# Channel mixer as seven block products instead of eight, with activations through DRAM

## The chip, the cores and the metric

The kernel runs on one core of a Trainium2 chip. The metric is the device time of one execution in microseconds. TensorE (PE) multiplies, VectorE (DVE), ScalarE (ACT) and GpSimd (POOL) work on elements, SyncE (SP) issues nearly all DMAs. Each engine takes its instructions in the order of its own queue.

## What is computed

One encoder layer and a final norm are applied to two sequences with the same weights, one of 512 tokens (short) and one of 1024 (long). Everything is float32.

```python
u = rms_norm(x, norm1_g)
proj = u @ w_in
...                                        # Fourier mixing and retention branches, gated and merged
x = x + merged @ w_out
u2 = rms_norm(x, norm2_g)
h_gate, h_val = jnp.split(u2 @ w_up, 2, axis=-1)          # 1024 -> 2 x 2816
h_conv = hp[:, :-2] * conv_w[0] + hp[:, 1:-1] * conv_w[1] + hp[:, 2:] * conv_w[2] + conv_b
x = x + (jax.nn.gelu(h_conv, approximate=False) * h_val) @ w_down   # 2816 -> 1024
y = rms_norm(x, final_norm_g)
```

`hp` is `h_gate` padded by one token at both ends. The change concerns the part from `u2` on, the channel mixer.

## The kernel before

Activations lie with the features on partitions and 512 tokens on the free axis. There are three such token tiles t: 0 is the short sequence, 1 and 2 are the long one. Each feature block k has 128 features, so D_MODEL is KD = 8 blocks and D_FF is FF = 22.

Each float32 operand is split into two parts of a shorter format, h (a ScalarE cast) and l (VectorE's subtraction `x - h`), by `split`, L71 and L72. `mm3` (L105 to L107) makes one product of 128 x 128 weights with 512 columns from three matmuls, hh, lh and hl. Weights come as slabs of 128 x 1024 (`wslab`): one DMA into `wr` and one split.

The merge runs over token tiles in the order 1, 2, 0: eight projections with w_ret_proj (RP), then eight with w_out (WO), each of 24 matmuls. `norm2` then makes the 16 split operands u2 of a token tile; it runs between the next tile's projections (`pend`).

The mixer runs over two groups, tiles (1, 2) and then tile 0. `up` makes one of the 22 feature blocks: the gate slab, the convolution (L786, L793, L796), the Gelu, the value slab, the product (L804) and its split. `down` takes two such blocks at a time, multiplies them by all eight output blocks and adds the result to y (L851); in the group's last call it also makes the squares for the final norm. `final` (L823) scales y and stores it. A down call stands in the code between the two up calls of the next pair, so that TensorE has other products while an activation is made. A scheduler orders the instructions of all engines by priority and by its own estimate of when each can run; the order is fixed when the program is built. Pools have a number of buffers; a tile waits for the buffer's earlier user.

Of the kernel before, what the change touches and what calls it, by code (L numbers as in the profile page):

```python
# [14 lines left out]
P = 128  # L15
# [10 lines left out]
SL_RP, SL_WO, SL_UP, SL_DN = 44, 52, 60, 104  # L26
N_SLABS = 126
# [6 lines left out]
def emit(ctx, tc, x, wsl, wfour, tab, cst, rcst, vec, out):  # L34
# [4 lines left out]
    upool = ctx.enter_context(tc.tile_pool(name="u", bufs=24))  # L39
# [34 lines left out]
    state = {}  # L74
# [29 lines left out]
    def mm3(o, lh, ll, rh, rl, first, last):  # L104
        nc.tensor.matmul(o, lh, rh, start=first, stop=False)  # L105
        nc.tensor.matmul(o, ll, rh, start=False, stop=False)  # L106
        nc.tensor.matmul(o, lh, rl, start=False, stop=last)  # L107
# [46 lines left out]
    # ------------------------------------------------------------- norm 1 and the mixers  # L154
    wpool = ctx.enter_context(tc.tile_pool(name="w", bufs=4, reuse_waits="tile"))
# [71 lines left out]
    # Fourier: channel DFT token-major, then the sequence DFT of the lower half of the frequencies  # L227
# [123 lines left out]
    # decays: per-head tables from the logits  # L351
# [139 lines left out]
    # retention, two heads at a time; the small steps run between thirds of the projections  # L491
# [225 lines left out]
    ntp = ctx.enter_context(tc.tile_pool(name="nt", bufs=4, reuse_waits="tile"))  # L717
    state["tmp"] = ntp, "nt", 4
    mp = cctx.enter_context(tc.tile_pool(name="mh", bufs=KD, side="right", reuse_waits="tile"))
    u2 = [None] * 3  # L720

    def norm2(t, xs, ss):
        r = rstd_cols(ss.acc)
        yield
        ps = rstd_rows(r)
        u2[t] = ([], [])
        for k in range(KD):
            s = tmp("xn")
            nc.vector.scalar_tensor_tensor(s, xs[k], vc[:, V_G2 + k:V_G2 + k + 1], ps, op0=ALU.mult, op1=ALU.mult)  # L729
            xs[k] = None  # L730
            h, l = utile("uh"), utile("ul")
            u2[t][0].append(h)
            u2[t][1].append(l)
            split(h, l, s)

    pend = None
    for it, t in enumerate(order):
        mh, ml = [], []
        for n in range(KD):
# [34 lines left out]
    pool = {}

    def up(gi, j):
        dp = pool["d"]
        ts = groups[gi]
        n = len(ts) * TC
        w = wslab(SL_UP + 2 * j)  # L780
        hc = dp.tile([P, 2 * TC], F32, name="hc", tag="hc", bufs=2)
        cw = [vc[:, V_CW + 3 * j + i:V_CW + 3 * j + i + 1] for i in range(3)]
        hps = []
        for i, t in enumerate(ts):
            ps = proj(w, u2[t])
            nc.scalar.activation(hc[:, i * TC:(i + 1) * TC], ps, AF.Identity,  # L786
                                 bias=vc[:, V_CB + j:V_CB + j + 1], scale=cw[1])
            hps.append(ps)
        for i, ps in enumerate(hps):
            o = i * TC  # L790
            e = min(o + TC + 1, n)
            s = hc[:, o + 1:e]
            nc.vector.scalar_tensor_tensor(s, ps[:, :e - o - 1], cw[0], s, op0=ALU.mult, op1=ALU.add)  # L793
            b = max(o - 1, 0)
            s = hc[:, b:o + TC - 1]
            nc.vector.scalar_tensor_tensor(s, ps[:, b + 1 - o:TC], cw[2], s, op0=ALU.mult, op1=ALU.add)  # L796
        nc.scalar.activation(hc[:, :n], hc[:, :n], AF.Gelu)
        w = wslab(SL_UP + 2 * j + 1)
        al = dp.tile([P, 2 * TC], F32R, name="al", tag="al", bufs=3)
        ah = dp.tile([P, 2 * TC], F32R, name="ah", tag="ah", bufs=3)  # L800
        for i, t in enumerate(ts):
            ps = proj(w, u2[t])
            m = slice(i * TC, (i + 1) * TC)
            nc.vector.tensor_tensor(hc[:, m], ps, hc[:, m], op=ALU.mult)  # L804
        split(ah[:, :n], al[:, :n], hc[:, :n])
        return ah, al

    def final(t, m, ss, fast):
# [7 lines left out]
        rr = pool["d"].tile([P, 2 * TC], F32, name="hc", tag="hc", bufs=2)[:, :cols]  # L816
        nc.scalar.copy(rr, ps[:, :cols])
        for n in range(KD):
# [3 lines left out]
            else:  # L822
                nc.gpsimd.tensor_tensor(y, y, rr, op=ALU.mult)  # L823
            nc.sync.dma_start(out[t, n, :, m], y)

    late = []

    def tick():
        for it in list(late):
            if next(it, late) is late:  # L830
                late.remove(it)

    def down(gi, b, acts):
        dp = pool["d"]
        ts = groups[gi]
        ws = [wslab(SL_DN + 2 * b + i) for i in range(2)]
        last = b == FF // 2 - 1
        units = [(i * TC, t, slice(0, TC)) for i, t in enumerate(ts)]
        if last and gi:
            units = [(0, 0, slice(0, TC // 2)), (TC // 2, 0, slice(TC // 2, TC))]  # L840
        for o, t, tm in units:
            cols = tm.stop - tm.start
            m = slice(o, o + cols)
            ss = SumSq()
            for n in range(KD):
                c = slice(n * P, (n + 1) * P)
                ps = bank(cols)
                for q in range(2):
                    mm3(ps, ws[q][0][:, c], ws[q][1][:, c], acts[q][0][:, m], acts[q][1][:, m], q == 0, q == 1)
                y = ys[t, n][:, tm]  # L850
                nc.vector.tensor_tensor(y, ps, y, op=ALU.add)  # L851
                if last:
                    ss.add(y)
                    nc.scalar.activation(y, y, AF.Identity, scale=vc[:, V_GF + n:V_GF + n + 1])
                if n % 2 or last:
                    tick()
# [4 lines left out]
    for gi in range(2):  # L861
        for b in range(FF // 2):
# [11 lines left out]
            if todo:  # L874
                down(*todo)
# [114 lines left out]
```

## Time and profile before

| what | us |
|---|---|
| median of 3 runs (lowest, highest) | 2377.97 (2377.53, 2379.83) |
| span of the profiled execution | 2379.3 |
| its time beside the span | no separate time is listed; the span lies inside the range of the runs |
| TensorE busy | 2340.7 |
| VectorE busy | 1192.4 |
| ScalarE busy | 651.3 |
| GpSimd busy | 368.4 |

The page gives the busy time of each engine, its share of the span and the number of instructions. Below it and in the groups, a row has the line in the kernel, the engine, the operation, out<-in by the program's names with shapes, the count, the busy time and the mean duration in ns, and the idle time ahead with what ended it. In a row by stretches, the columns are the length, then the busy time and the count of each engine, then TensorE's granted clock, the share of the DMA engines and GB/s. Rows in order of time have the start, the duration, the engine and the instruction.

### The profile page before, as it was taken

What the parts mean: (1) busy time and instruction counts of PE and PEld (TensorE: products, weight loads), DVE (VectorE), ACT (ScalarE), POOL (GpSimd) and SP (SyncE); (2) the same over time, 40 slices, a digit from 0 to 9 for tenths busy, and PEclk for the clock granted to TensorE, in tenths of its full rate; (3) what the DMA queues carried; (4) which work ended last, traced back from release to release, by engine and by line L of the source; (5) the groups of instructions that cost most, each with busy time, mean ns of one, the idle gap of its engine ahead of it and who ended that gap; (6) DMA issues with size and microseconds to landing.
All of it is one profiled execution on the core that took longest, in us unless ns stands there. A gap on an engine that the chain in (4) does not pass through costs nothing.

```text
span 2379.3 us, 27499 instructions
## 1 busy us (share of the span) xinstructions
PE 2340.7 (98%) x10898; PEld 1918.6 (81%) x10898; DVE 1192.4 (50%) x2144; ACT 651.3 (27%) x1007; POOL 368.4 (15%) x200
## 2 busy tenths in 40 slices
PE   8899999999999999999999999999999999999997
PEld 6788888888888888877878788888888888788886
DVE  7454435656555642456543643444443446555555
ACT  6242222222222212234332211112211215322323
POOL 3799401212111110101100000000000002200000
PEclk9999999999999999999999999999999999999999
DMA  5252220201011123557453111111111113423231
GB/s 182 72 165 89 81 70 1 80 1 54 27 45 36 40 81 115 186 183 236 144 185 119 48 50 45 42 48 53 48 50 45 47 51 114 143 89 106 89 98 62
DMA packets 76593, 203.46 MB, mean 86 GB/s; under 512 B 8496, under 2 KB 11824, under 8 KB 76464
## 3 DMA queue, kind: packets, MB, share of 16 engines
q1 hardware_dynamic: 73008, 195.41, 26.0%
q10 hardware_dynamic: 3456, 6.29, 0.7%
q8 instruction: 86, 1.41, 0.2%
q14 instruction: 43, 0.35, 0.0%
HBM read 170.21 MB, written 31.46 MB: 85 GB/s over the span
## 4 chain that ended last, share of the span: by engine, by line
PE 87%; DVE 3%; DMA 2%; ACT 2%; POOL 1%; issue 1%; SPq 0%; POOLq 0%; ACTq 0%; DVEq 0%
PE bank L105 27%; PE bank L106 27%; PE bank L107 27%; DMA wr<-wsl 2%; PE bank L616 1%; DVE wl L72 1%; PE bank L562 1%; PE bank L573 1%; PE bank L569 1%; ACT wh L71 1%; POOL y L823 1%; DMA og<-og 1%; PE bank L551 1%; PE bank L638 0%; DVE xn L729 0%
## 5 line engine op out<-in xcount | busy, mean ns | idle before, releaser
L105 PE MATMUL bank<-uh,wh 128*128 128x512 f32 x1728 | 688.3, 398 | 5.0 <-ACT wh L71 5.0
L107 PE MATMUL bank<-ul,wh 128*128 128x512 f32 x1728 | 683.9, 396 | 0.0
L106 PE MATMUL bank<-uh,wl 128*128 128x512 f32 x1728 | 683.2, 395 | 0.2 <-DVE wl L72 0.2
L71 ACT CAST wh<-wr 128x1024 fp32r<-128x1024 f32 (+3 forms) x256 | 258.1, 1017 | 743.9 <-PE bank L107 626.5
L105 PEld LDWEIGHTS bank<-uh,wh 128*128 128x128 f32 x1728 | 325.4, 188 | 79.1 <-ACT wh L71 5.0
L106 PEld LDWEIGHTS bank<-uh,wl 128*128 128x128 f32 x1728 | 325.4, 188 | 75.8 <-DVE wl L72 1.2
L107 PEld LDWEIGHTS bank<-ul,wh 128*128 128x128 f32 x1728 | 325.2, 188 | 75.6
L72 DVE TENSOR_TENSOR wl<-wr,wh 128x1024 fp32r<-128x1024 f32 (+3 forms) x256 | 313.2, 1231 | 95.1 <-ACT wh L71 93.4
L851 DVE TENSOR_TENSOR y<-bank,y 128x512 f32<-128x512 f32 (+1 forms) x272 | 178.8, 674 | 115.3 <-PE bank L107 114.3
L105 PE MATMUL bank<-ah,wh 128*128 128x512 f32 (+1 forms) x544 | 211.9, 390 | 1.0 <-DVE y L851 0.7
L106 PE MATMUL bank<-ah,wl 128*128 128x512 f32 (+1 forms) x544 | 211.0, 388 | 1.1 <-DVE wl L72 1.1
L107 PE MATMUL bank<-al,wh 128*128 128x512 f32 (+1 forms) x544 | 210.2, 387 | 0.0
L129 POOL TENSOR_TENSOR nr<-nv,mhalf 128x4 f32<-128x4 f32 (+1 forms) x10 | 11.9, 1194 | 1180.1 <-DVE nv L128 1149.8
L793 DVE SCALAR_TENSOR_TENSOR hc<-bank,vc,hc 128x512 f32<-128x512 f32 (+1 forms) x66 | 47.5, 748 | 260.3 <-ACT hc L786 260.3
L420 POOL TENSOR_TENSOR D<-two,D 128x64 f32<-128x64 f32 x16 | 170.3, 10675 | 0.0
L105 PE MATMUL bank<-wh,uh 128*128 128x512 f32 x384 | 166.8, 434 | 0.0
L106 PE MATMUL bank<-wh,ul 128*128 128x512 f32 x384 | 151.6, 395 | 0.0
L107 PE MATMUL bank<-wl,uh 128*128 128x512 f32 x384 | 151.2, 394 | 0.0
L804 DVE TENSOR_TENSOR hc<-bank,hc 128x512 f32<-128x512 f32 x66 | 45.6, 692 | 171.4 <-PE bank L107 170.1
L786 ACT ACTIVATE hc<-bank,vc 128x512 f32<-128x512 f32 x66 | 51.4, 779 | 273.5 <-PE bank L107 273.5
L105 PEld LDWEIGHTS bank<-ah,wh 128*128 128x128 f32 x544 | 102.3, 188 | 24.5 <-DVE y L851 1.1
L106 PEld LDWEIGHTS bank<-ah,wl 128*128 128x128 f32 x544 | 102.3, 188 | 23.9 <-DVE wl L72 1.8
(172 smaller groups left out, 2861.4 us busy)
## 6 DMA issues: line engine op xcount, KB each, us to landing
wr<-wsl SPq DMA_DIRECT2D x222, 512.0 KB, 3.7
wr<-tab SPq DMA_DIRECT2D x18, 516.0 KB, 3.7
xs<-x SPq DMA_DIRECT2D x24, 256.0 KB, 4.7
sb<-sg ACTq DMA_DIRECT2D x24, 256.0 KB, 2.0
ma<-sg SPq DMA_DIRECT2D x24, 256.0 KB, 2.0
og<-sg SPq DMA_DIRECT2D x24, 256.0 KB, 2.4
og<-og SPq DMA_DIRECT2D x24, 256.0 KB, 3.9
uh<-x SPq DMA_DIRECT2D x24, 256.0 KB, 4.0
```

What stands on the lines that cost most here:

```text
L71: nc.scalar.copy(h, src)
L72: nc.vector.tensor_tensor(l, src, h.bitcast(F32), op=ALU.subtract)
L105: nc.tensor.matmul(o, lh, rh, start=first, stop=False)
L106: nc.tensor.matmul(o, ll, rh, start=False, stop=False)
L107: nc.tensor.matmul(o, lh, rl, start=False, stop=last)
L420: nc.gpsimd.tensor_tensor(D[:, m], two.broadcast_to([P, 64]), D[:, m], op=ALU.pow)
L551: nc.tensor.transpose(tp[:, i * P:(i + 1) * P], r[:, i * P:(i + 1) * P], ident)
L562: nc.tensor.matmul(sp, kT, qbd.rearrange("p h n -> p (h n)"), start=True, stop=True)
L786: nc.scalar.activation(hc[:, i * TC:(i + 1) * TC], ps, AF.Identity, bias=vc[:, V_CB + j:V_CB + j + 1], scale=cw[1])
L793: nc.vector.scalar_tensor_tensor(s, ps[:, :e - o - 1], cw[0], s, op0=ALU.mult, op1=ALU.add)
L804: nc.vector.tensor_tensor(hc[:, m], ps, hc[:, m], op=ALU.mult)
L851: nc.vector.tensor_tensor(y, ps, y, op=ALU.add)
```

## The change

A product of two matrices cut into 2 x 2 blocks is made from seven block products and 15 block sums instead of eight products (Winograd's form). The blocks of the weights are halves of the contraction and halves of the outputs. The blocks of the activations are halves of the contraction and halves of the tokens: for the long sequence, tiles 1 and 2; for the short one, columns 0 to 255 and 256 to 511.

- `u_ops(k)` loads x2 of the long sequence again, scales it, and makes seven split operands for block pair k and k+4 (A11, A12, A22, S1 to S4). Blocks 0 and 1 run in the third merge's RP part, 2 in its WO part, 3 behind it. `u_ops0(k)` does that for the short sequence.
- `w_ops` loads one 128 x 2048 slab (w_up's gate and value blocks for one j, both contraction halves) and makes three sums and the splits, so that seven weight operands are there. They are made anew for each sequence.
- `quad` runs the seven products into three banks and hands the results to a `sink` as they come. `quads` chains jobs: the first product of a job stands ahead of the last two of the job before.
- The long sequence runs its 22 up jobs first. `spill_pair` stores two activations and their four sums in DRAM (`da` to `dd`). Then the down projection runs in four groups of 2, 3, 3 and 3 pairs, four jobs each; `act_ops` loads and splits seven operands for each pair, and the sinks add to y.
- The short sequence then runs 22 up jobs with 256 columns, keeps all activations, and its down projection runs by output block over 20 activations, then the last two by half tiles as before.
- The finals of the long sequence run between the short one's up jobs, one scaling per step.

```diff
+OPS = ("A11", "S1", "S2", "A12", "S3", "S4", "A22")
+DN_GROUPS = ((0, 2), (2, 5), (5, 8), (8, 11))
...
+    def w_ops(src, w):
+        raw = wp.tile([P, 2048], F32, name="wr", tag="wr", bufs=2)[:, :4 * w]
+        nc.sync.dma_start(raw, src)
...
+        b11, b21 = hl(raw[:, :2 * w], 2)
+        ta = wp.tile([P, 1024], F32, name="wt", tag="wt", bufs=2)[:, :2 * w]
+        nc.vector.tensor_tensor(ta.rearrange("p (b c) -> p b c", b=2), b[:, 2:4], b[:, 0:3:2], op=ALU.subtract)
+        t1, t3 = hl(ta, 2)
+        tb = wp.tile([P, 1024], F32, name="wt", tag="wt", bufs=2)[:, :2 * w]
+        nc.vector.tensor_tensor(tb[:, :w], b[:, 3], ta[:, :w], op=ALU.subtract)
+        nc.vector.tensor_tensor(tb[:, w:], b[:, 1], tb[:, :w], op=ALU.subtract)
+        t2, t4 = hl(tb, 2)
+        b22, = hl(b[:, 3], 1)
...
+    def quad(w, act, cols, sink):
+        a = bank(cols)
+        product(a, w, act, "A11", start=True)
+        sink("P1", a)
+        yield
+        c = bank(cols)
+        product(c, w, act, "S1", start=True)
+        product(a, w, act, "S2")
+        sink("P1+P6", a)
+        b = bank(cols)
+        product(b, w, act, "A12", start=True)
+        sink("P2", b)
+        product(a, w, act, "S3")
+        sink("P1+P6+P7,P5", (a, c))
+        yield
+        product(c, w, act, "S4")
+        sink("P5+P3", c)
+        product(a, w, act, "A22")
+        sink("P1+P6+P7+P4", a)
+        yield
...
+    def spill_pair(j, a):
...
+        nc.sync.dma_start(d[0], a0[:, lo])
+        nc.sync.dma_start(d[1], a1)
+        s12 = tp.tile([P, 2 * TC], F32, name="v", tag="v")
+        nc.vector.tensor_tensor(s12[:, lo], a0[:, hi], a1[:, hi], op=ALU.add)
+        nc.vector.tensor_tensor(s12[:, hi], s12[:, lo], a0[:, lo], op=ALU.subtract)
+        nc.sync.dma_start(d[2], s12)
+        s34 = tp.tile([P, 2 * TC], F32, name="v", tag="v")
+        nc.vector.tensor_tensor(s34[:, lo], a0[:, lo], a0[:, hi], op=ALU.subtract)
+        nc.vector.tensor_tensor(s34[:, hi], a1[:, lo], s12[:, hi], op=ALU.subtract)
+        nc.sync.dma_start(d[3], s34)
...
+    for _ in quads([up_job(tp, j, uop, TC, spill_pair) for j in range(FF)]):
+        pass
...
+    def act_ops(p):
+        ops = {}
+        for name in OPS:
+            l, h = optile(p % 4), optile(p % 4)
+            nc.sync.dma_start(l.bitcast(F32), opd[p][name])
+            nc.scalar.copy(h, l.bitcast(F32))
+            nc.vector.tensor_tensor(l, l.bitcast(F32), h.bitcast(F32), op=ALU.subtract)
...
+    state["tmp"] = yp, "nt", 4
...
+    def u_ops0(k):
...
+        for kk in (k, k + 4):
+            v = tmp("x0")
+            nc.sync.dma_start(v, x2_d[kk][0])
+            nc.vector.scalar_tensor_tensor(v, v, vc[:, V_G2 + kk:V_G2 + kk + 1], rr[0], op0=ALU.mult, op1=ALU.mult)
...
+        s12, s34 = tmp("s12"), tmp("s34")
...
+    for _ in quads(down_jobs()):
+        pass
+    for k in range(4):
+        u_ops0(k)
+    for t in (1, 2):
+        late.append(final((yp, "fr", 1), t, slice(0, TC), state["sums"][t], ()))
...
+    for j, _ in enumerate(quads([up_job(t0p, j, uop0, H, keep) for j in range(FF)])):
...
```

The order of the instructions changes nearly everywhere in the mixer. Three places matter here.

VectorE in the short sequence's up projection. Before, two feature blocks and the down call of the pair before them take eight y sums, four more slabs and two chains of convolution, product (L804) and split (`al`):

```order
L851 TENSOR_TENSOR y<-bank,y 128x512 x8
L72 TENSOR_TENSOR wl<-wr,wh 128x1024 x2
L793 SCALAR_TENSOR_TENSOR hc<-bank,vc,hc 128x511
L796 SCALAR_TENSOR_TENSOR hc<-bank,vc,hc 128x511
L72 TENSOR_TENSOR wl<-wr,wh 128x1024
L804 TENSOR_TENSOR hc<-bank,hc 128x512
L72 TENSOR_TENSOR wl<-wr,wh 128x1024
L72 TENSOR_TENSOR al<-hc,ah 128x512
```

After, one job, thus one feature block, has these and two more (a 256-wide sink L953 and the split `w4l`); L804, L807 and L808 are the sums of weight blocks, L948 and L951 sinks, L959 the product:

```order
L804 TENSOR_TENSOR wt<-wr 128x1024
L75 TENSOR_TENSOR wl<-wr,wh 128x1024
L932 SCALAR_TENSOR_TENSOR hc<-g,vc,hc 128x511
L807 TENSOR_TENSOR wt<-wr,wt 128x512
L933 SCALAR_TENSOR_TENSOR hc<-g,vc,hc 128x511
L948 TENSOR_TENSOR g<-bank,g 128x256
L808 TENSOR_TENSOR wt<-wr,wt 128x512
L75 TENSOR_TENSOR wl<-wt,wh 128x1024
L959 TENSOR_TENSOR hc<-v,hc 128x512
L951 TENSOR_TENSOR v<-bank,v 128x256
L75 TENSOR_TENSOR wl<-wt,wh 128x1024
L75 TENSOR_TENSOR al<-hc,ah 128x512
```

The y sums are gone from this stretch, and weight splits and sums of weight blocks stand in their place.

VectorE between the long and the short sequence. Before, the last y sums and squares of the long one mix with the short one's first slabs and its first feature block:

```order
L851 TENSOR_TENSOR y<-bank,y 128x512
L72 TENSOR_TENSOR wl<-wr,wh 128x1024
L152 TENSOR_TENSOR sq<-sq 128x512 x2
L72 TENSOR_TENSOR wl<-wr,wh 128x1024
L793 SCALAR_TENSOR_TENSOR hc<-bank,vc,hc 128x511
L796 SCALAR_TENSOR_TENSOR hc<-bank,vc,hc 128x511
L804 TENSOR_TENSOR hc<-bank,hc 128x512
```

After, the first block of `u_ops0` (L1069 the scaling, L1076 to L1079 the sums, L75 the splits) follows on the last y sums (L1029) and some weight work, and three more such blocks follow on it:

```order
L808 TENSOR_TENSOR wt<-wr,wt 128x512
L1069 SCALAR_TENSOR_TENSOR x_15319<-x_15319,vc,rr_8230 128x512
L1069 SCALAR_TENSOR_TENSOR x_15322<-x_15322,vc,rr_8230 128x512
L75 TENSOR_TENSOR op<-x_15319,op 128x256
L1076 TENSOR_TENSOR s_15328<-x_15319,x_15322 128x256
L1078 TENSOR_TENSOR s_15329<-x_15319 128x256
L1077 TENSOR_TENSOR s_15328<-s_15328,x_15319 128x256
L1079 TENSOR_TENSOR s_15329<-x_15322,s_15328 128x256
L75 TENSOR_TENSOR op<-s_15328,op 128x512
L75 TENSOR_TENSOR op<-x_15322,op 128x512
L75 TENSOR_TENSOR op<-s_15329,op 128x512
L1069 SCALAR_TENSOR_TENSOR x_15346<-x_15346,vc,rr_8230 128x512
```

The four blocks stand behind the long sequence's last sum; no other work stands between them.

SyncE's queue between the long up and the long down projection. Before there is no such border; the loads of y stand between stores of x2 and slabs at the start of the mixer:

```order
L88 DMA wr<-wsl 128x1024
L766 DMA xx_0_167<-uh 128x512
L88 DMA wr<-wsl 128x1024
L873 DMA y<-xx_1_150 128x512
L766 DMA xx_0_170<-uh 128x512
L873 DMA y<-xx_1_153 128x512
```

After, loads of operands (`op`) stand among stores of the last pair and ahead of the 16 loads of y, of which the first three are shown:

```order
L1047 DMA op<-db_10469 128x512
L977 DMA db_10505<-hc 128x1024
L1047 DMA op<-dd_10471 128x512
L981 DMA dc_10506<-v 128x1024
L985 DMA dd_10507<-v 128x1024
L1047 DMA op<-dd_10471 128x512
L1057 DMA y<-xx_1_150 128x512
L1057 DMA y<-xx_1_162 128x512
L1057 DMA y<-xx_2_151 128x512
```

The operands of the first group now share the queue with stores that wait for VectorE and with the loads of y.

More of the change, by code (lines that the diff above doesn't have):

```diff
@@ new lines, in emit, with tick, quads @@
+    late = []
+    def tick():
+        for it in list(late):
+            if next(it, late) is late:
+                late.remove(it)
+    def quads(jobs):
+        prev = None
+        for prep, act, cols, sink, after in jobs:
+            w = prep()
+            g = quad(w, act, cols, sink)
+            next(g)
+            if prev:
+                next(prev[0])
+                prev[1]()
+                tick()
+            next(g)
+            tick()
+            prev = g, after
+            yield
+        next(prev[0])
+        prev[1]()
+        tick()
@@ L767, in emit @@
             ss.add(xr)
-            xs.append(xr)
-        pend = norm2(t, xs, ss)
-    groups = ((1, 2), (0,))
-    ys = {}
[L774 to L806, printed above, removed]
@@ L808, in final, with dspill @@
-    def final(t, m, ss, fast):
+            if pend and next(pend, 0) == 0:
+                pend = None
+        if it < 2:
+            pend = chain(norm2(t, ss), *((u_ops(0), u_ops(1)) if it else ()))
+    for _ in pend or ():
+        pass
+    mctx.close()
+    homes[3] = right("opc", 14, occtx)
+    for _ in u_ops(3):
+        pass
+    late.append(norm2(0, ss))
+    nctx.close()
+    def dspill(name, cols):
+        return dram.tile([P, cols], F32, name=name, tag=name)
+    opd = []
+    for p in range(FF // 2):
+        first, second, s12, s34 = dspill(f"da{p}", TC), *(dspill(f"d{x}{p}", 2 * TC) for x in "bcd")
+        opd.append({"A11": first, "A12": second[:, :TC], "A22": second[:, TC:], "S1": s12[:, :TC],
+                    "S2": s12[:, TC:], "S3": s34[:, :TC], "S4": s34[:, TC:], "tiles": (first, second, s12, s34)})
@@ L822, in final @@
             else:
-                nc.gpsimd.tensor_tensor(y, y, rr, op=ALU.mult)
+                nc.gpsimd.tensor_tensor(y, y, rw, op=ALU.mult)
             nc.sync.dma_start(out[t, n, :, m], y)
[L826 to L856, printed above, removed]
-            if last:
-                late.append(final(t, tm, ss, range(5) if gi else ()))
@@ new lines, in down_jobs @@
+    def down_jobs():
+        sums = None
+        for gi, (p0, p1) in enumerate(DN_GROUPS):
+            pairs = [act_ops(p) for p in range(p0, p1)]
+            act = {name: [o[name] for o in pairs] for name in OPS}
+            if gi == len(DN_GROUPS) - 1:
+                sums = {1: SumSq(rr[1]), 2: SumSq(rr[2])}
+            for q in range(4):
+                yield down_job(gi, q, act, sums)
+        state["sums"] = sums
+    for _ in quads(down_jobs()):
+        pass
+    for k in range(4):
+        u_ops0(k)
@@ new lines, in emit, with keep @@
+    for t in (1, 2):
+        late.append(final((yp, "fr", 1), t, slice(0, TC), state["sums"][t], ()))
+    occtx.close()
+    obctx.close()
+    actx = ExitStack()
+    t0p = right("t0", 2, actx)
+    ap = [(right("act", 22, actx), "act", 22), None, (opa, "op", 28)]
+    acts = [None] * FF
+    def keep(j, a):
+        pool, tag, bufs = ap[0 if j < 11 else 1 if j < 20 else 2]
+        l, h = (pool.tile([P, TC], F32R, name=x, tag=tag, bufs=bufs) for x in ("al", "ah"))
+        split(h, l, a)
+        acts[j] = h, l
@@ new lines, in emit @@
+    ws = [wslab(SL_DL + i) for i in range(2)]
+    for m in (slice(0, H), slice(H, TC)):
+        ss = SumSq()
+        for n in range(KD):
+            c = slice(n * P, (n + 1) * P)
+            ps = bank(H)
+            for q in range(2):
+                mm3(ps, ws[q][0][:, c], ws[q][1][:, c], acts[20 + q][0][:, m], acts[20 + q][1][:, m],
+                    q == 0, q == 1)
+            y = ys[0, n][:, m]
+            nc.vector.tensor_tensor(y, ps, y, op=ALU.add)
+            y_done(0, n, m, ss)
+            tick()
+        late.append(final((opa, "op", 28), 0, m, ss, range(5)))
```

271 lines of the change are left out of this document (215 added, 56 removed).

## Prediction

> **What bounds the kernel now.** I read the page first, then the busy time by stretches, then TensorE's own rows in the channel mixer.
>
> ```profile
> span 2379.3 us, 27499 instructions
> ...
> PE 2340.7 (98%) x10898; PEld 1918.6 (81%) x10898; DVE 1192.4 (50%) x2144; ACT 651.3 (27%) x1007; POOL 368.4 (15%) x200
> ```
> ```profile
> core 0: us, PE busy (x) PEld busy (x) DVE busy (x) ACT busy (x) POOL busy (x), PEclk, DMA share, GB/s
> 1249.26:2351.19 1101.93, 1099.81 (x4753) 889.08 (x4752) 520.53 (x660) 276.78 (x326) 28.47 (x19) 1.00 0.23 71
> 1160.00:1204.60 44.60, 44.60 (x201) 36.38 (x201) 28.51 (x37) 15.91 (x22) 12.31 (x8) 1.00 0.59 190
> 1204.60:1249.26 44.66, 43.72 (x188) 34.75 (x186) 20.84 (x25) 12.99 (x17) 0.00 (x0) 1.00 0.47 153
> 1400.00:1900.00 500.00, 500.00 (x2153) 404.32 (x2152) 210.17 (x268) 98.06 (x105) 0.00 (x0) 1.00 0.15 48
> ```
>
> From 1249.26 us, where the mixer's up projection starts, to 2351.19, where the last half-width unit starts, TensorE has 1099.81 of 1101.93 us and VectorE 520.53, under half. So this stage costs what its matmuls cost, and the price of one is the distance between two starts, not the mean duration, which overlaps its neighbour:
>
> ```profile
> 1249.26 0.39 PE L105 MATMUL bank<-uh,wh 128*128 128x512 f32 x1
> ...
> 1254.85 0.40 PE L105 MATMUL bank<-uh,wh 128*128 128x512 f32 x1
> ```
> ```profile
> 2351.19 0.28 PE L105 MATMUL bank<-ah,wh 128*128 128x256 f32 x1
> ...
> 2359.25 0.28 PE L107 MATMUL bank<-al,wh 128*128 128x256 f32 x1
> ```
>
> The first pair is 24 matmuls of 512 columns apart: 0.2329 us each; 2153 in 500 us give 0.2322. I use 0.2325. The second pair is 67 matmuls of 256 columns apart: 0.120 us each, though each loads its own weights.
>
> **The change, part by part.** VectorE's prices come from the mixer's groups:
>
> ```profile
> L851 DVE TENSOR_TENSOR y<-bank,y 128x512 f32<-128x512 f32 x256 | 172.5, 690 | 114.1 <-PE bank L107 113.1
> L72 DVE TENSOR_TENSOR wl<-wr,wh 128x1024 fp32r<-128x1024 f32 x123 | 150.2, 1234 | 31.4 <-ACT wh L71 31.4
> ...
> L796 DVE SCALAR_TENSOR_TENSOR hc<-bank,vc,hc 128x511 f32<-128x511 f32 x41 | 30.6, 746 | 0.8
> ...
> L72 DVE TENSOR_TENSOR al<-hc,ah 128x512 fp32r<-128x512 f32 x22 | 15.3, 694 | 2.1 <-ACT ah L71 2.1
> ...
> L851 DVE TENSOR_TENSOR y<-bank,y 128x256 f32<-128x256 f32 x16 | 6.3, 420 | 1.2 <-PE bank L107 1.2
> ...
> L72 DVE TENSOR_TENSOR ul<-xn,uh 128x512 fp32r<-128x512 f32 x8 | 5.1, 688 | 0.0
> L729 DVE SCALAR_TENSOR_TENSOR xn<-uh,vc,bank 128x512 f32<-128x512 f32 x6 | 4.1, 744 | 0.0
> ```
>
> Widths between these go by the 0.54 us that 512 more columns cost: 768 takes 0.96, 384 takes 0.55.
>
> *Matmuls, the gain.* Before, the mixer has 3 token tiles x (44 x 8 + 22 x 8) x 3 = 4752 matmuls of 512 (the last 96, of half width, counting as 48). The long sequence's up projection goes from 2112 to 22 x 84 = 1848: 264 x 0.2325 = 61.4 us less. Its down projection goes from 1056 to 924: 30.7 us less. The short sequence's up projection goes from 1056 of 512 columns (245.5 us) to 1848 of 256 (1848 x 0.120 = 221.8): 23.7 us less. Its down projection keeps its count. Together 115.8 us, all on TensorE, which sets the end. What follows takes part of it back.
>
> *The long up job.* One job is 84 x 0.2325 = 19.5 us of TensorE. VectorE has three 1024-wide splits and one difference of that width (4 x 1.23), a 512 split and two 512 differences (2.07), three sinks (2.07), two 1023-wide steps of the convolution (0.746 + 0.53 each by the slope from 512 to 1024, 2.6), a 1024 product (1.23), and half of four 512-wide sums for the stores (1.4): 14.3 us. It fits, so does ScalarE's, whose 1024-wide casts are its largest part, and the 1.9 MB of traffic per job; I cost these at nothing. Without that cover the most it could lose is 14.3 against 19.5, still none.
>
> *Third merge.* The two rows from 1160 show VectorE at 49.4 of 89.3 us. Its eight norm steps and splits there (8 x (0.744 + 0.688) = 11.5) go, three blocks of operands come (each 4 x 0.75 + 11 x 0.69 = 10.6). About 70 of 89 fits; the first half is fuller, and the fourth block waits for the last projection to free its buffers. 0 to 8 us; I take 4, as TensorE has three ready quarters of the first product meanwhile.
>
> *Start of the long down projection, and its groups.* A group job of three pairs is 63 x 0.2325 = 14.6 us of TensorE. VectorE: w_ops at 768 columns 5.5, seven sinks 4.8, 21 splits per four jobs 3.6: 14.0, nearly as much. At the start the order puts the splits of pairs 2 and 3 ahead of pair 1's, on SyncE's queue too, behind stores that wait for VectorE and 16 loads of y. From the P2 sink of the last up job VectorE has some 28 us of work before the first y sum, and TensorE only 8.4 us of up work and 2.8 of ready first halves. Walking the two queues against each other, TensorE idles about 2, 5 and 1 us there and 5 in all at the three later borders: 14 us. Bounds: 4 (only the first hole) and 35 (two holes of 5 us at every border).
>
> *Between long down and short up.* All four blocks of u_ops0 stand on VectorE behind the last y sum. Each has two 0.75 steps, five of 256 columns (0.42) and three 512 splits: 5.7 us. Its scratch is four buffers, all of them used by one block, so the next block's load waits for them:
>
> ```profile
> og<-og SPq DMA_DIRECT2D x24, 256.0 KB, 3.9
> ...
> y<-xx SPq DMA_DIRECT2D x24, 256.0 KB, 4.9
> ```
>
> A 256 KB load of this kind lands after 3.9 to 4.9 us; 3.3 us of the next block follow before its own second input is free, so a block takes some 7.1 to 7.5 us. Four of them, 4 us of VectorE's earlier work and 4.5 us of the remaining products end the first job 35.5 us after the long down, where its matmuls and the next product need 11.5. Cost 24 to 25, taken 25; bounds 16 (loads hidden: 4 x 5 us) and 34 (4.9 us loads, in row with the work).
>
> *The short up job.* TensorE has 84 x 0.120 = 10.1 us. VectorE: 4 x 1.234 + 0.694 + 2 x 0.69 + 3 x 0.42 + 2 x 0.746 + 0.69 + 0.694 = 11.15 us in 14 instructions. Is that the price? Rows back to back say less:
>
> ```profile
> 1996.39 0.69 DVE L851 TENSOR_TENSOR y<-bank,y 128x512 f32<-128x512 f32 x1
> 1997.00 1.48 DVE L152 TENSOR_TENSOR sq<-sq 128x512 f32<-128x512 f32 x2
> ```
>
> An instruction of 0.69 us is followed after 0.61. I take 0.07 off each: 14 x 0.07 = 1.0, so 10.15 us, level with TensorE. With some waiting on ScalarE's casts I take 10.5 a job: 22 x 0.42 = 9 us over the matmuls. Bounds: 0, and 24 at the full 11.15.
> The Trainium skill (VectorE: DVE Perf Modes, The DRAIN you can't avoid) says that the next instruction starts only when the pipe of the one before has emptied. The 0.61 above speaks against it for these pairs, and by it this part would be 24 us.
>
> *GpSimd beside VectorE.* The 16 final scalings of the long sequence now run beside the short up jobs. What that did before:
>
> ```profile
> L823 POOL TENSOR_TENSOR y<-y,hc 128x512 f32<-128x512 f32 x8 | 13.4, 1712 | 3.1 <-ACT hc L817 3.1
> ...
> L72 DVE TENSOR_TENSOR wl<-wr,wh 128x1024 fp32r<-128x1024 f32 x2 | 3.9, 1966 | 0.0
> ```
>
> In that stretch (1998.3 to 2012 us) a 1024 split took 1.966 us and not 1.234. 16 x 1.712 = 27.4 us of GpSimd, 37% of VectorE's time lost in them, on the three quarters of its work that read two SBUF tensors: 8 us. Bounds 0 and 27.
> The Trainium skill (SBUF — State Buffer, on the port pair that VectorE and GpSimd share) has the later of two such instructions blocked outright; that would be towards the upper bound, and the 1.966, not the sum of both durations, agrees only in part.
>
> *Short down and tail.* Same matmuls; each 5.6 us weight part needs one 1.23 us split, hidden. The first split and the loads of y: 0 to 6, taken 3.
>
> Sum: 4 + 14 + 25 + 9 + 8 + 3 = 63 lost of 115.8, a gain of 52.8: 2379.3 - 52.8 = 2326.5. The span of the profile stands 1.3 us above the runs' median of 2377.97, so I say 2325.
>
> **Rivals.**
> A: VectorE is hidden nearly everywhere. Only the low ends for the starts, 4 + 16, are lost: 2378 - 95.8 = 2282. For it: VectorE's sums never pass TensorE's by more than 1.1 us a job. Against: the u_ops0 block stands alone.
> B: VectorE's instructions cost their full durations. Short up 24 instead of 9, u_ops0 and the transition some 10 more: 2325 + 25 = 2350. For it: a start behind a wait on ScalarE overlaps nothing.
> This is also what the rule of VectorE: DVE Perf Modes in the Trainium skill, cited above, would make of it.
> C, on the other side: VectorE's queue paces the short up jobs, with a wait at nearly each of its 14 instructions, since they alternate between ScalarE's casts and TensorE's products. The gain is gone when a job takes 10.5 + 53/22 = 12.9 us, which is 0.13 us of waiting per instruction on top of full durations; at 13.4 us it is 2325 + 64 = 2389, slower. Against: TensorE's products run four ahead of the weights they need.
> D: the 256-column matmuls do not come at 0.120 but at their weight loads' pace. Line groups give loads 188 ns:
>
> ```profile
> L107 PEld LDWEIGHTS bank<-ul,wh 128*128 128x128 f32 x960 | 180.4, 188 | 42.3
> ```
>
> 1848 x 0.188 = 347, 126 us more: 2451. The 67 matmuls at 0.120, each with a load, speak against it.
>
> **How the numbers follow.** My forecast has 0.52 (its own range 2310 to 2342), B 0.20, A 0.14, C 0.10, D 0.01; 0.03 lies between C and my case. 0.2% is 4.8 us, about what runs of this kernel can tell from no change. Faster: 0.52 + 0.20 + 0.14 and 0.01 of the rest, 0.87; same 0.02; slower 0.11. For 8 in 10 the range takes in my case, B with its bounds (to 2370) and the upper part of A: 2290 to 2370.
>
> **What would show it.** Matmuls of 512 in the long stage 0.23 us apart with TensorE near 19.5 us a job: the gain is right. One hole of some 24 us on TensorE between the last 512-wide down product and the short up jobs: u_ops0. Short jobs 10.5 us apart with VectorE over 90% busy there: the pace; under 10.2 is A, 11.2 is B, over 12.9 is C. VectorE's 1024 splits near 2 us in the first four of these jobs: GpSimd. The prediction fails most easily if the in-order queues of SyncE and ScalarE hold TensorE at each group of the down projection, which I only walked by hand at the first.

## The result, and the profile after

The changed kernel takes 2325.56 us (median of 4 runs, 2323.36 to 2328.64) against 2378.9 us of four runs before: a ratio of 0.9774, 95% interval 0.976 to 0.9788, faster. The forecast was 2325, in 2290 to 2370. The number is right, and three of the terms behind it are not; that is what this part is about.

The page of the changed kernel, its first line and the busy times:

```profile
span 2326.9 us, 29230 instructions
...
PE 2248.8 (97%) x11294; PEld 1880.7 (81%) x11294; DVE 1478.9 (64%) x2539; ACT 849.1 (36%) x1373; POOL 374.3 (16%) x200
```

The span is 52.4 us shorter than before. TensorE is busy 91.9 us less, VectorE 286.5 us more. By stretches (length, then each engine's busy time and count, TensorE's granted clock, DMA share, GB/s):

```profile
1204.77:1253.95 49.18, 46.21 (x193) 36.98 (x192) 39.17 (x51) 18.84 (x26) 1.67 (x1) 0.97 0.64 211
1253.95:1684.00 430.05, 428.50 (x1848) 344.99 (x1847) 301.97 (x342) 184.98 (x237) 1.40 (x1) 1.00 0.28 101
1684.00:1720.00 36.00, 24.49 (x73) 16.26 (x72) 27.54 (x45) 13.99 (x24) 0.00 (x0) 0.76 0.82 286
1720.00:1926.00 206.00, 203.30 (x872) 162.49 (x870) 176.46 (x270) 89.52 (x138) 0.00 (x0) 1.00 0.37 123
1926.00:1951.60 25.60, 12.38 (x44) 9.95 (x43) 22.86 (x43) 10.77 (x21) 0.00 (x0) 0.60 0.39 113
1951.60:2016.00 64.40, 52.58 (x399) 51.97 (x400) 55.84 (x64) 31.27 (x52) 31.35 (x18) 0.90 0.38 132
2016.00:2187.00 171.00, 171.00 (x1427) 171.00 (x1426) 168.16 (x236) 113.99 (x188) 0.00 (x0) 1.00 0.30 101
2187.00:2299.78 112.78, 112.78 (x496) 91.76 (x495) 34.10 (x39) 23.44 (x28) 0.00 (x0) 1.00 0.36 110
```

They are, in order: the third merge's second half, the long up projection, the start of the long down projection, the rest of it, its border to the short up projection, jobs 1 to 5 of that, its other jobs, the short down projection. Behind the merge TensorE loses most in three places: 1684 to 1720, 1926 to 1951.6 and 1951.6 to 2016. Elsewhere it is nearly full.

The long up jobs are 19.55 us apart, the short ones 10.08 from job 6 on. The distance from one job to the next is read from the first product on the fourth weight operand (`w4`), for instance:

```profile
2157.03 0.28 PE L110 MATMUL bank<-op,w4h 128*128 128x256 f32 x1
2167.11 0.28 PE L110 MATMUL bank<-op,w4h 128*128 128x256 f32 x1
2177.20 0.28 PE L110 MATMUL bank<-op,w4h 128*128 128x256 f32 x1
```

**The start of the long down projection.** The up products end at 1688.14 us. Up to 1721.14, the first down job's first `w4` product (an expectation below calls it job 2's), 58 matmuls run, 13.5 us of work in 33.0: 19.5 us lost. TensorE's waits between 1684 and 1722 us (sum, times, longest), and its rows in order of time:

```profile
PE bank L110 <- DVE y L1029: 4.2, 2, 3.4
PE bank L112 <- DVE op L1049: 3.6, 3, 2.3
PE bank L110 <- ACT op L1048: 1.6, 1, 1.6
```
```profile
1698.54 0.54 PE L110 MATMUL bank<-op,wh 128*128 128x512 f32 x1 [1.59 <-ACT op L1048]
1698.88 0.63 PE L111 MATMUL bank<-op,wl 128*128 128x512 f32 x1
1701.79 0.80 PE L112 MATMUL bank<-op,wh 128*128 128x512 f32 x1 [2.28 <-DVE op L1049]
...
1707.29 0.63 PE L110 MATMUL bank<-op,wh 128*128 128x512 f32 x1
1707.72 0.63 PE L111 MATMUL bank<-op,wl 128*128 128x512 f32 x1
1708.15 0.63 PE L112 MATMUL bank<-op,wh 128*128 128x512 f32 x1
1712.20 0.56 PE L110 MATMUL bank<-op,wh 128*128 128x512 f32 x1 [3.43 <-DVE y L1029]
```

All waits together are 11.4 us. Most of the rest is in rows like the three without a wait: the matmuls start 0.43 us apart, not 0.2325. 23 of them do so, some 4.6 us (the expectations of e6 and e7 below take 7 to 8), in the stretch with a granted clock of 0.76. That 0.76 is a mean; inside it the clock is lower:

```profile
1700.00:1708.00 8.00, 5.51 (x12) 4.03 (x13) 5.35 (x9) 1.14 (x2) 0.00 (x0) 0.50 0.91 290
```

The last wait is for a y sum. The 16 loads of y start at 1703.24, behind the last stores of activations, and land 5.1 to 6.0 us after they are issued. VectorE's first y sum starts at 1711.47:

```profile
1703.24 10.54 SPq L1057 DMA_DIRECT2D y<-xx  x16
```
```profile
1709.46 0.69 DVE L75 TENSOR_TENSOR wl<-wt,wh 128x512 fp32r<-128x512 f32 x1 [4.12 <-ACT wh L74]
...
1711.47 1.41 DVE L1029 TENSOR_TENSOR y<-bank,y 128x512 f32<-128x512 f32 x2
```
```profile
1708.81 0.62 ACT L74 CAST wh<-wt 128x512 fp32r<-128x512 f32 x1 [5.05 <-PE bank L112]
```

The sum does not start when its load lands. It stands in VectorE's queue behind a split of weights that waited 4.12 us for ScalarE, which had waited 5.05 us for TensorE's slow matmuls. The loads set a lower limit, and the order of the queue added to it.

**Between long down and short up.** One border of 22.7 us, as forecast: 6.0 between 1925.68 and 1931.86, and 16.7 inside the first job (25.3 us to its first `w4`, for 72 matmuls or 8.6 us). VectorE's blocks start 6.1 us apart:

```profile
1936.17 0.75 DVE L1069 SCALAR_TENSOR_TENSOR x<-x,vc,rr 128x512 f32<-128x512 f32 x1 [0.22 <-DMA x<-xx]
...
1942.28 0.75 DVE L1069 SCALAR_TENSOR_TENSOR x<-x,vc,rr 128x512 f32<-128x512 f32 x1
...
1948.43 0.75 DVE L1069 SCALAR_TENSOR_TENSOR x<-x,vc,rr 128x512 f32<-128x512 f32 x1
```

The loads, 2.4 to 2.8 us here, are waited for 0.2 us once. It is VectorE's own work and its waits for ScalarE's casts that set the 6.1.

**Jobs 4 to 6 of the short up projection.** 45.1 us where three jobs are 30.2: 14.8 us lost. VectorE, GpSimd, ScalarE and TensorE there:

```profile
1977.55 1.22 DVE L75 TENSOR_TENSOR wl<-wt,wh 128x1024 fp32r<-128x1024 f32 x1
...
1979.63 2.28 DVE L75 TENSOR_TENSOR wl<-wt,wh 128x1024 fp32r<-128x1024 f32 x1
1981.83 1.78 DVE L75 TENSOR_TENSOR al<-hc,ah 128x512 fp32r<-128x512 f32 x1
...
1985.77 0.41 DVE L953 TENSOR_TENSOR v<-bank,v 128x256 f32<-128x256 f32 x1
```
```profile
1979.54 13.70 POOL L1012 TENSOR_TENSOR y<-y,fr 128x512 f32<-128x512 f32 x8 [7.50 <-ACT fr L1006]
```
```profile
1993.27 0.59 ACT L1006 COPY fr<-bank 128x512 f32<-128x512 f32 x1 [10.10 <-POOL y L1012]
```
```profile
1996.38 0.58 PE L110 MATMUL bank<-op,wh 128*128 128x256 f32 x1 [8.10 <-ACT v L946]
```

Two explanations stand in these rows. Read along the waits: TensorE waits for ScalarE, ScalarE for GpSimd, since the scale row `fr` has one buffer; an in-order queue is held. Read by durations: VectorE's split that starts with GpSimd's scalings takes 2.28 us and not 1.22. The experiments separate them.

### The profile page after: what moved, and what is told of

It is laid out like the page before. It is cut to its first block, busy times and chain, and to the rows that moved or that the text cites. A ratio compares the mean times of both kernels' runs of the same rounds, so it can differ in the third digit from the quotient of the medians.

```text
span 2326.9 us, 29230 instructions
## 1 busy us (share of the span) xinstructions
PE 2248.8 (97%) x11294; PEld 1880.7 (81%) x11294; DVE 1478.9 (64%) x2539; ACT 849.1 (36%) x1373; POOL 374.3 (16%) x200
## 5 line engine op out<-in xcount | busy, mean ns | idle before, releaser
L110 PE MATMUL bank<-op,wh 128*128 128x512 f32 (+1 forms) x1320 | 468.7, 357 | 35.2 <-ACT op L74 13.0
L112 PE MATMUL bank<-op,wh 128*128 128x512 f32 (+1 forms) x1320 | 466.5, 355 | 4.2 <-DVE op L1049 3.6
L111 PE MATMUL bank<-op,wl 128*128 128x512 f32 (+1 forms) x1320 | 468.1, 355 | 0.9 <-DVE wl L75 0.9
L75 DVE TENSOR_TENSOR wl<-wr,wh 128x1024 fp32r<-128x1024 f32 (+5 forms) x210 | 250.5, 1194 | 189.1 <-ACT wh L74 187.2
L74 ACT CAST wh<-wr 128x1024 fp32r<-128x1024 f32 (+5 forms) x210 | 204.7, 976 | 327.6 <-PE bank L112 237.1
L110 PEld LDWEIGHTS bank<-op,wh 128*128 128x128 f32 x1320 | 254.6, 193 | 78.8 <-ACT op L74 15.2
L112 PEld LDWEIGHTS bank<-op,wh 128*128 128x128 f32 x1320 | 254.3, 193 | 42.2 <-DVE op L1049 5.2
L111 PEld LDWEIGHTS bank<-op,wl 128*128 128x128 f32 x1320 | 255.1, 193 | 36.3 <-DVE wl L75 1.3
L110 PE MATMUL bank<-uh,wh 128*128 128x512 f32 x672 | 272.3, 405 | 5.0 <-ACT wh L74 5.0
L112 PE MATMUL bank<-ul,wh 128*128 128x512 f32 x672 | 266.6, 397 | 0.0
L111 PE MATMUL bank<-uh,wl 128*128 128x512 f32 x672 | 266.4, 396 | 0.0
L112 PEld LDWEIGHTS bank<-ul,wh 128*128 128x128 f32 x672 | 126.9, 189 | 29.6
L75 DVE TENSOR_TENSOR wl<-wt,wh 128x1024 fp32r<-128x1024 f32 (+2 forms) x120 | 138.5, 1154 | 11.0 <-ACT wh L74 10.9
```

Of the source, the lines that this page charges most:

```text
L74: nc.scalar.copy(h, src)
L75: nc.vector.tensor_tensor(l, src, h.bitcast(F32), op=ALU.subtract)
L110: nc.tensor.matmul(o, lh, rh, start=first, stop=False, skip_group_check=go_on)
L111: nc.tensor.matmul(o, ll, rh, start=False, stop=False, skip_group_check=go_on)
L112: nc.tensor.matmul(o, lh, rl, start=False, stop=last, skip_group_check=go_on)
```

## The experiments

All are edits of the changed kernel. Beside the times stands a stretch of the trace that leaves out what varies ahead of the mixer: from the first matmul of 256 columns to the first half-tile product of the short down projection, 367.9 us in the changed kernel.

**Who holds jobs 4 to 6?** Four edits of the final scalings.

```diff
-        late.append(final((yp, "fr", 1), t, ...))
+        late.append(final((yp, "nt", 4), t, ...))          # e1: a row for each tile
-            nc.sync.dma_start(out[t, n, :, m], y)
+            (nc.sync if fast else nc.gpsimd).dma_start(out[t, n, :, m], y)   # e2: stores; e3: both
-        late.append(final(..., state["sums"][t], ()))
+        late.append(final(..., state["sums"][t], range(KD)))     # e4: on VectorE
```

> The changed kernel, but the scale rows of tiles 1 and 2 lie in two buffers instead of one, so that ScalarE no longer stands 10.1 us behind GpSimd's eight scalings with the second copy of such a row. In the changed kernel the jobs 4 to 6 of the short up projection take 45.1 us from the fourth operand product of job 3 to that of job 6, where three jobs are 30.2: 14.8 us lost. Theory S (in-order holds: ScalarE's copy, and at the same time SyncE's stores, which wait for GpSimd and stand ahead of a weight load): freeing one of two holds that end together changes little; here ten stores now stand ahead of the weight load, so it is issued some 8 us later. Expected 2322 to 2334, the three jobs 43 to 55 us. Theory H (ScalarE's hold alone): 9 us less, about 2316. Theory V (GpSimd slows VectorE: its instructions in 1979 to 2009 us took 11.8 us longer than elsewhere): within 2 us of 2325.6.

> The changed kernel, but the sixteen stores of tiles 1 and 2 are issued by GpSimd behind its scalings instead of by SyncE, so no store stands ahead of a weight load. ScalarE still waits for the one buffer of the scale row. Theory S: ScalarE's hold ends at the same moment as the weight load's landing did, so nothing is gained: 2323 to 2328. If SyncE's hold alone was the cause: 9 us less, about 2316. Theory V: within 2 us of 2325.6.

> Both edits: two buffers for the scale rows and the stores on GpSimd's queue. Theory S: the hole of 8.4 us ahead of job 4 goes and most of the 3.8 us behind it: the three jobs take 33 to 36 us, time 2314 to 2317. Theory V: GpSimd still runs 28 us beside VectorE and slows each of its instructions with two SBUF operands by 0.75 to 1.1 us; VectorE is the busier engine there (10.1 us of work in a 10.1 us job), so its 12 us stay: three jobs 42 to 44 us, 2323 to 2325.

> The changed kernel, but the sixteen final scalings run on VectorE (scale row read from PSUM) and not on GpSimd: no engine shares the SBUF with VectorE there, and neither hold can arise. VectorE gets 16 x 0.61 = 9.8 us more. Both theories: the 14.8 us go and up to 9.8 come back, as VectorE has hardly any slack: 2320 to 2322. If VectorE has slack in the short jobs, down to 2311.

| run | us (range) | ratio to before (95%) | stretch | lost in jobs 4 to 6 |
|---|---|---|---|---|
| changed kernel | 2325.56 (2323.36, 2328.64) | 0.9774 (0.976, 0.9788) | 367.9 | 14.8 |
| e1, two buffers | 2324.81 (2322.93, 2327.17) | 0.9771 (0.9754, 0.9787) | 366.1 | 13.0 |
| e2, stores on GpSimd | 2325.64 (2325.19, 2329.24) | 0.9776 (0.9762, 0.9791) | 369.0 | 15.9 |
| e3, both | 2328.48 (2326.7, 2331.72) | 0.9787 (0.9772, 0.9801) | 370.6 | 17.7 |
| e4, on VectorE | 2324.95 (2322.52, 2327.4) | 0.977 (0.9756, 0.9785) | 367.8 | spread over all jobs |

e1 takes ScalarE's wait of 10.1 us away and brings 1.8 us, not 9: theory H falls. With both holds gone (e3) the loss is not smaller but larger, so theory S falls too. The 47.9 us of e3's three jobs are also more than theory V's 42 to 44; no run shows why the scalings cost more when GpSimd issues the stores as well. What e3 shows instead of the holds, TensorE, VectorE and then GpSimd:

```profile
1995.89 0.58 PE L111 MATMUL bank<-op,wl 128*128 128x256 f32 x1 [7.73 <-DVE wl L75]
```
```profile
1987.51 3.63 DVE L807 TENSOR_TENSOR wt<-wr,wt 128x512 f32<-128x512 f32 x1
1991.18 3.52 DVE L808 TENSOR_TENSOR wt<-wr,wt 128x512 f32<-128x512 f32 x1
```
```profile
1988.10 2.49 POOL L1012 TENSOR_TENSOR y<-y,fr 128x512 f32<-128x512 f32 x2
1990.52 1.12 POOL L1013 DMA_DIRECT2D out<-y  x2
1991.65 2.48 POOL L1012 TENSOR_TENSOR y<-y,fr 128x512 f32<-128x512 f32 x2
```

An instruction of 0.68 us takes 3.63: it ends 0.55 us after a pair of GpSimd's instructions has ended (1988.10 + 2.49 = 1990.59, and 1991.14), and the next one does the same. That looks like an engine that stands still while the pair runs, not like one that runs slower. Its sums out of PSUM, with one operand in SBUF, keep their 0.41 us (in the changed kernel the row at 1985.77, in the middle of eight scalings). That is the rule in the Trainium skill (SBUF — State Buffer, Who interferes with whom): an exclusive lock between a GpSimd instruction that reads SBUF and a VectorE one with two SBUF inputs. These rows agree with it.

e4 is inconclusive on its own: it moved VectorE's whole order in the short stage, with a wait of 0.43 us for a cast in each job, and its jobs came 10.55 us apart. It does not show what 16 scalings cost on VectorE.

Theory V then needs the suspect taken away with all else in place. GpSimd's scalings are cut to 16 columns:

```diff
-                nc.gpsimd.tensor_tensor(y, y, rw, op=ALU.mult)
+                nc.gpsimd.tensor_tensor(*((y, y, rw) if fast else
+                                          (y[:, :16], y[:, :16], rw[:, :16])), op=ALU.mult)
```

> The changed kernel, but GpSimd's sixteen final scalings of the long sequence touch 16 of 512 columns each (496 columns of each output block are left unscaled); the order of TensorE's and VectorE's instructions stays. Theory V (GpSimd blocks VectorE): the 14.8 us of jobs 4 to 6 go, VectorE's instructions in them have the durations of the later jobs, three jobs take 30.2 to 31.5 us, time 2310 to 2313. If anything else in these jobs was the cause (TensorE's banks, the norm's small matmuls, the weights' loads): three jobs stay above 36 us.

2310.35 us (2307.71 to 2312.63), ratio 0.971 (0.9695, 0.9724); the stretch is 354.8, and the three jobs take 31.8 us. VectorE beside GpSimd in that run:

```profile
1972.15 1.22 DVE L75 TENSOR_TENSOR wl<-wt,wh 128x1024 fp32r<-128x1024 f32 x1
1973.28 0.71 DVE L75 TENSOR_TENSOR al<-hc,ah 128x512 fp32r<-128x512 f32 x1
```

So GpSimd is the cause of 13.3 of the 14.8 us (45.1 less 31.8). Shorter scalings also end both holds sooner, so it takes e1 to e3 as well to say that it works mostly not through the queues: freeing the holds brings 1.8 us at most. A chain of waits that is true row by row named the wrong thing.

**The start of the long down projection.** Pairs 0 and 1 shared a pool whose tiles come free with the last up products; pairs 2 and 3, not needed yet, had pools of their own and were split first. e6 swaps the pools. e7 also gives the first job's four y tiles space of their own.

```diff
-            l, h = optile(p % 4), optile(p % 4)
+            l, h = optile((p + 2) % 4), optile((p + 2) % 4)      # e6, e7
...
-    yp = left("y", 1, yctx)
+    ntp, yp, ya = left("ntp", 1, yctx), left("y", 1, yctx), left("ya", 1, yctx)   # e7
...
-                ys[t, n] = yp.tile(..., tag="y", bufs=16)
+                ys[t, n] = (yp if q else ya).tile(..., tag="y", bufs=12 if q else 4)
```

> The changed kernel, but pairs 0 and 1 of the long down projection take their operand tiles from the two separate pools of 14 and pairs 2 and 3 from the shared pool of 28 (before, the other way round), so that both pairs of the first group can be loaded as the last up products free tiles, and VectorE splits them ahead of pairs 2 and 3. In the changed kernel the start of the down projection loses 19.5 us (33.0 us from the end of the up products to the first product on the fourth weight operand of job 2, for 13.5 us of matmuls); 5.2 us of waits are for operands, 4.2 for y sums, and about 8 us are matmuls 0.43 us apart instead of 0.2325. Theory O (late operands): 19.5 becomes 8 to 13, time 2314 to 2319. Theory Y (the y loads, issued from 1703 us on, set the first y sum and thereby when banks come free): the wait only moves, 17 to 20 us stay, 2323 to 2326.

> As the run before, and the four y tiles of the first down job lie in space of their own, so that they are loaded long before. Theory Y, and theory O with it: the first y sums follow the first products, 19.5 becomes 3 to 8 us, time 2309 to 2314. The granted clock: if waits bring it down, it stays at 1.0 from 1684 to 1720 us and no matmuls there are 0.43 us apart; if it falls for another reason (the load of all engines at that border), they stay, and 7 us with them.

e6: 2325.32 us (2323.96 to 2326.7), ratio 0.9771 (0.9755, 0.9788): the same as without it, as theory Y had it. TensorE no longer waits for operands (`op`), but for a split of weights in their place, and as long as before for the y sum:

```profile
PE bank L111 <- DVE wl L75: 3.8, 1, 3.8
PE bank L110 <- DVE y L1029: 3.6, 1, 3.6
```

e7: 2319.25 us (2317.73 to 2320.14), ratio 0.9747 (0.9732, 0.9761), 6.3 less. From the `w4` product of long up job 21 to the first short matmul it takes 258.5 us; the changed kernel and the runs that leave this part alone take 263.4 to 267.3, and e6 264.7. Its stretch from 1684 to 1720:

```profile
1684.00:1720.00 36.00, 31.77 (x124) 23.57 (x123) 33.38 (x56) 15.34 (x27) 0.00 (x0) 0.95 0.71 249
```

124 matmuls instead of 73, at a clock of 0.95 instead of 0.76; nine are still 0.43 us apart instead of 23. VectorE and ScalarE are busier in it than before (33.38 and 15.34 us, not 27.54 and 13.99), so this speaks for the waits as what brings the clock down, and against the load of the engines; it does not show it, since no run made such waits alone. e7 also changed VectorE's order, which can be part of the gain: the first y sum now stands ahead of the last convolution.

```profile
1688.72 0.68 DVE L1029 TENSOR_TENSOR y<-bank,y 128x512 f32<-128x512 f32 x1
1689.32 1.27 DVE L932 SCALAR_TENSOR_TENSOR hc<-g,vc,hc 128x1023 f32<-128x1023 f32 x1
```

What the early loads bring by themselves, and what the order that came with them, is not separated. The expectation, 2309 to 2314, was too good: one wait of 2.6 us for a y sum stays at the start, and from 1710 us on TensorE waits 5.3 us for others, where the changed kernel has 2.7 from 1722 on.

**Is the short up projection worth it?** e8 makes it by ordinary products.

```diff
-    for j, _ in enumerate(quads([up_job(t0p, j, uop0, H, keep) for j in range(FF)])):
+    for j in range(FF):
+        pg = proj(slab(wup[j][:, :1024]), u0)
+        hc = conv_gelu(t0p, j, pg, TC)
+        tick()
+        pv = proj(slab(wup[j][:, 1024:]), u0)
+        nc.vector.tensor_tensor(hc, pv, hc, op=ALU.mult)
+        keep(j, hc)
```

> The changed kernel with the short sequence's up projection made by ordinary products again (two slabs of 1024 columns per job, 48 matmuls of 512 columns, operands of eight blocks without sums); the long sequence as changed. By the measured terms: 23.7 us of matmuls come back; VectorE has some 5.3 us of work in a job of 11.2, so GpSimd's scalings cost 0 to 3 instead of 14.8 us; the operands take 8 x 1.3 = 10.5 us of VectorE instead of 23, so the hole of 22.7 becomes 8 to 12. Sum: 23.7 - 12 to 14.8 - 11 to 15: 2319 to 2326, that is, seven products for the short up projection are worth nothing. If they are worth their matmuls: 2340 to 2349.

2314.17 us (2312.79 to 2316.22), ratio 0.9727 (0.9712, 0.9741): 11.4 us faster than with seven products, and below the range. 23.7 us of saved matmuls cost more than they bring, because VectorE becomes the equal of TensorE there. In e8 GpSimd's 14.8 us vanish (from 1935 to 1990 us, beside all 16 scalings, VectorE is busy 21.4 of 55 us and TensorE 54.0), and the border shrinks to two waits for operands in the short stage, 5.5 us together:

```profile
PE bank L110 <- ACT op L74: 5.5, 2, 4.9
```

That holds for this order of the work, not for seven products as such: e9 below, which keeps them and makes two of the four blocks of operands early, is no slower than e10 with ordinary ones (2304.38 against 2308.5 us, with ranges that overlap). Seven products with all their operands made early and without GpSimd's scalings were not run.

**The border, and the two best versions.** With the slots of e6, 14 tiles are free while the last down group runs. e9 makes two of the four blocks of `u_ops0` there; e11 does it with six of the eight plain operands. e10 is e8 with e7.

```diff
             for q in range(4):
                 yield down_job(gi, q, act, sums)
+                if gi == len(DN_GROUPS) - 1 and q < 2:
+                    u_ops0(q)                       # e9
...
-    for k in range(4):
+    for k in range(2, 4):
         u_ops0(k)
```

> The run with the new slots and early y tiles (2319.25 us), and two of the four operand blocks of the short sequence's up projection are made while the long sequence's last down group runs; the 14 tiles that they need are free there by the new slots. In that run TensorE loses 22.4 us between the last long product and job 2 of the short up projection. Theory U (VectorE's work for four blocks, 5.7 to 6.1 us each in a row, is the hole): two blocks go from the hole, 10 to 12 us less, VectorE has 1 us free in 7 in the last down group and 3 to 5 us of the work show up there: 2310 to 2314. If the hole is set by the loads or by ScalarE's other work behind the last sum: within 3 us of 2319.

> Ordinary products for the short up projection, with the new slots and the early y tiles for the long down projection. The two gains lie in different stages: 2314.2 - 6.3 = 2308, range 2305 to 2310. If the gain at the start of the down projection is given back at a later border: 2312 to 2315.

> As the run before, and six of the eight operands of the short up projection are made during the long sequence's last down group. Behind the last product TensorE waited 4.9 us for the first operand and 0.9 us later. Theory U: 3 to 6 us less than the run before. If VectorE's 8 us more in the last group delay its sums: the same as the run before, or up to 3 us more.

e9: 2304.38 us (2302.74 to 2306.82), ratio 0.9679 (0.9665, 0.9694). It gained 14.9 us on e7's median, and 12.3 in the trace from the `w4` product of long up job 21 to that of the last short job, the part that the edit touches: theory U, without the price expected in the last group. e10: 2308.5 us (2305.05 to 2311.28), 0.9695 (0.968, 0.971), as expected. e11: 2297.2 us (2294.53 to 2299.89), 0.9648 (0.9634, 0.9663), the fastest version. It gained 11.3 instead of 3 to 6, because with the wait of 4.9 us went a wait of 1.5 ahead of it and 14 matmuls 0.43 us apart behind it. TensorE at the border, in e11:

```profile
1908.00:1925.00 17.00, 17.00 (x76) 13.87 (x75) 13.15 (x18) 10.24 (x15) 0.00 (x0) 1.00 0.42 125
```

**How near is VectorE to being the bound?** One more instruction of 0.68 us in each short job from the seventh on:

```diff
+        for _ in range(more):
+            nc.vector.tensor_tensor(tb[:, w:], b[:, 1], tb[:, :w], op=ALU.subtract)
```

> The changed kernel with one more VectorE instruction in the short up jobs 7 to 22 (the second half of the second weight sum, 128 x 512, is made twice; the result is the same). In the changed kernel these jobs are 10.08 us apart, which is TensorE's 84 x 0.120, and VectorE's 14 instructions follow each other with 0.2 us of gaps per job. Theory P (VectorE is within 0.2 us of being the bound): 10.5 us per job, 16 x 0.42 = 6.5 us more, 2331 to 2333. If VectorE has slack that the trace does not show as idle: 10.1 us per job, 2324 to 2327.

2336.08 us (2334.26 to 2337.48), ratio 0.9813 (0.9797, 0.983). The jobs come 10.8 us apart, and the time is 3 to 5 us above the expectation: theory P, and 0.3 more than its 10.5. The order around the instruction changed as well, and VectorE waits about 0.24 us for a cast. The stretch from 2050 to 2150 us, which TensorE filled before:

```profile
2050.00:2150.00 100.00, 98.06 (x782) 94.56 (x783) 97.57 (x139) 61.93 (x102) 0.00 (x0) 1.00 0.28 96
```

## Why the prediction was right, point by point

| step | predicted us | measured us | shown by |
|---|---|---|---|
| long up job | 19.5 each | 19.55 | trace |
| third merge and before | -4 | -4.7 (0.5 to 5.5 in the other builds, which share this part) | trace |
| long up's waits, start of long down | -9 | -1.5 and -19.5 | trace; e6, e7 for the y loads |
| later group borders | -5 | -3.4 | trace |
| border to short up | -25 | -22.7 | e9 |
| pace of short up | -9 | 0 (10.08 and not 10.5) | trace, e12 |
| GpSimd beside VectorE | -8 | -14.8 | e5, against e1 to e3 |
| short down, tail | -3 | 0, and +1.0 in the last 27 us | trace |

The measured losses are 65.6 us; before, the same stage had 2.1 us of waits of its own (1101.93 - 1099.81) that went with it. 115.8 - 65.6 + 2.1 = 52.3, against 52.4 between the two spans. The gain in matmuls and the border to the short up projection were right. The rest is luck: two terms too small by 18.8 us together, against 16.9 too large in four others.

Two sums of the prediction do not come out. Its waits of 2, 5 and 1 us and 5 at the later borders make 13 us, not 14 (the 9 and 5 above share out the 14). Four blocks of 7.1 us with 4 and 4.5 us make 36.9 us, not 35.5. Neither changes the forecast by more than 1.4 us.

- **Start of long down, the step that was most wrong.** "Walking the two queues against each other, TensorE idles about 2, 5 and 1 us there". The walk followed VectorE's and TensorE's queues only. The y loads on SyncE's queue were named as being behind stores, but no time was given to them, and with the operands early the start gained nothing measurable until they were early too (e6, e7). The slow matmuls, 4.6 us here, had no term. What the prediction feared most, holds at each later group of the down projection, cost 3.4 us.
- **Pace.** "I take 0.07 off each", so 10.15 us for VectorE and 10.5 for the job. The 14 instructions follow each other in 9.9 us (10.08 less 0.2 of gaps), 0.08 off each, and they wait for almost nothing. This is the pace that rival A named (under 10.2); rivals B and C fall with it. The prediction gave only half of what the Trainium skill says of the emptying pipe (VectorE: DVE Perf Modes, The DRAIN you can't avoid): the same paragraph adds that "A next op that is not held starts earlier". These rows agree with that half, and the 24 us do not follow from the section as a whole.
- **GpSimd.** "37% of VectorE's time lost": the 1.966 us before was read as slower work. e3's 3.63 us looks like VectorE standing still for whole instructions of GpSimd. In the stretch before from which the 1.966 came, a row that the prediction left out was already longer by more, 1.209 us where such sums of squares take 0.68:

```profile
L152 DVE TENSOR_TENSOR sq<-sq 128x512 f32<-128x512 f32 x4 | 4.8, 1209 | 0.2
```

The prediction set the rule of the shared pair (SBUF — State Buffer, in the Trainium skill) aside as agreeing "only in part"; here the rule was the better guide to the mechanism, though 14.8 us lie nearer to the 8 than to its end of the range, 27.
- **Border.** Right in size, for a partly wrong reason: the loads land after 2.6 us and not 3.9 to 4.9, and 6.1 instead of 7.1 us a block is VectorE and ScalarE.
- Rival D is out: 1848 matmuls at 0.120 us.

- Rival A needed the start and the border near their lower ends, 4 and 16 us; they are at 22.9 with the later borders, and 22.7.

Left open: what exactly brings the clock down at the start of the long down projection (no run made such waits alone), how much of e7's gain is its new order, and how much of e12's extra 0.3 us is.

## What to carry to other kernels

A saving in matmuls that is paid for in sums and splits is worth its matmuls only while the other engine has slack: with VectorE busy 13.5 us in a job of 19.55 the long up projection kept all of it; with 9.9 in 10.08 the short one kept its pace, but lost the gain and more at its border and beside GpSimd. When a wait chain ends at an engine, compare the durations in it with those of the same instruction elsewhere before blaming a queue. And at a border between stages, follow the loads that the first result needs, not just the operands.

## What was not expected of the hardware

- TensorE's granted clock fell to 0.50 for 8 us, and to a mean of 0.76 over 36 us, in which no single wait was over 3.5 us; matmuls then started 0.43 us apart instead of 0.2325. The Trainium skill (TensorE: Matmul & The Clock Gate, HAM oscillation — how this bites in real kernels) gives idle gaps of more than about 3.4 us as the condition; here the slow rows begin at 1698.88 us, behind five waits of 0.4 to 1.6 us.
- A VectorE instruction of 0.68 us with two SBUF operands lasted 3.63 us beside two GpSimd instructions, and one that reads PSUM kept its 0.41.
- Back to back, 14 VectorE instructions took 1.15 us less than the sum of their durations (11.05).
